# A trunk's second PEER: two dense tiles and two gathered ones in plain float32, U and V rows in one gather

## The chip, the core and the metric

The kernel runs on one core of a Trainium2 chip. The metric is device time in microseconds (us); the time of a kernel is the median of its runs. The engines are TensorE (PE, with its weight loads shown apart as PEld), VectorE (DVE), ScalarE (ACT), GpSimd (POOL) and SyncE (SP). SP and POOL issue nearly all the DMAs, which 16 DMA engines carry out.

## What is computed

The reference is two layers of a transformer-like trunk over 512 latent tokens and 256 context tokens of 1024 features, in float32. Each layer is a mixer (pooling and convolution in layer 0; mLSTM and attention in layer 1) and then PEER, a retrieval of experts, each followed by a residual and a layer norm. In layer 1 only the 512 latent tokens go through PEER, as four tiles of 128 tokens. What PEER computes, cut to what matters:

```python
q = (hb @ w_q).reshape(128, 8, 2, 128)             # 8 heads, two halves of the key
s = einsum('nhpd,pkd->nhpk', q, sub_keys)          # 128 sub-keys for each half
sv, si = top_k(s, 16)                              # then the 16 best of the 16 x 16 sums
eidx, gate = ...                                   # 8 x 16 = 128 experts of 16384 for each token
act = gelu(einsum('nd,nhkd->nhk', hb, u_tab[eidx]))
return einsum('nhk,nhkd->nd', gate * act, v_tab[eidx])
```

The tables U and V have 16384 rows of 1024 float32 each, 64 MB a table. There are two ways to get a token's sum. The dense way multiplies all of U with the tokens, takes the GELU, multiplies by a matrix of gates that is zero except for the chosen experts, and multiplies all of V with that. The gathered way reads only the chosen rows: for each of the 128 choices (a "slot") one indirect DMA brings one row per token, 128 rows in all, and VectorE makes the dot product or adds the weighted row.

## The kernel before

Layer 0 (its mixer and `peer` with l = 0) comes first and the change leaves it as it is. Layer 1 is `mixer1`, whose end is the output projection `proj_out`, and then `peer` with l = 1 (lines 647 to 1100). There three tiles are dense and one (tile 3) is gathered.

Dense products are made with split operands: each float32 operand is cast by ACT to a float32r part (line 297) and DVE makes the remainder (line 298), and TensorE runs three products (hi hi, hi lo, lo hi) in place of one (`mm_chunk`, line 303; line 1070 for V). All PE products show line 69 in the profile, since a helper issues them.

The stages of `peer` in layer 1, in order:

- The query of the gathered tile (lines 926 to 941): 16 pieces of w_q, plain float32, 128 token columns; `scores` (line 705) takes the top 16 of 128 sub-keys on DVE. A piece's scores are issued two pieces later (`QL`).
- The query of the dense tiles and the U products (lines 944 to 972). `u_chunk` (line 911) loads one of 128 chunks of U on SP, splits it, runs 24 products of 384 columns, applies the GELU and stores the result `at` in DRAM (`A_d`). Behind each chunk, `back` (line 892) issues a portion of what the products do not wait for: the choice of experts (`select`, line 725), the gates of the dense tiles (`build`, line 794: ACT and DVE make one-hot rows, PE multiplies them, ACT copies, SP stores 1 MB pieces to `G_d`), and the gathered rows (`run_gather`). A planner's clocks, advanced by the costs in `COST`, decide how much.
- The V products (lines 1034 to 1085): for each chunk SP loads V (two chunks to a DMA), the stored activations (`ag`) and the gates (`gg`); POOL multiplies the two (line 1059), ACT and DVE split both operands, PE adds 18 products of 512 columns into the accumulators `res`. The rest of the gathered rows is spread over these chunks.
- The residual and norm of each tile, and the store of the output (lines 988 to 995).

`gather` (line 662) goes over the table U first, 128 slots of 4 KB rows, then over V, 128 more. POOL issues each indirect DMA (line 667) into one of six row buffers; DVE takes the dot product (line 671) or adds the row (line 675). An instruction on POOL, ACT or DVE waits for all that was issued before it on that engine. In the code, `tc.issue_after` only moves the place of an instruction in that order.

## Time and profile before

| | us |
|---|---|
| median of 3 runs | 3844.92 |
| lowest and highest run | 3842.33, 3851.66 |
| span of the profiled execution | 3842.2 |

No time of its own is listed for the profiled execution, so its span is taken as its time; it lies 2.7 us under the median. The profile gives for each engine the time in which it was busy, for each stretch the mean share in which the 16 DMA engines were busy and the rate in GB/s, and for each group of instructions the count, the busy time and the mean duration. The products are pipelined, so the mean duration of one is longer than the time from one to the next; that is read from the count in a stretch in which PE had no gap. A plain float32 product has two records in the trace, a float32r product one.

### The profile page before, as it was taken

The numbers are of one execution on the slowest core, as the hardware profiler recorded it, in microseconds if no ns is written. First come the engines' busy times: TensorE is split into PE (matmuls) and PEld (weight loads), VectorE is DVE, ScalarE is ACT, GpSimd is POOL, SyncE is SP. The second block draws the span as 40 slices with busy tenths as digits, with TensorE's granted clock in tenths as the row PEclk, the third lists the DMA queues.
The fourth block names the chain that finished last, engine by engine and source line by source line (L and its number), as shares of the span: only waits on it lengthen the run. The fifth ranks groups of instructions, "written<-read, shape, count | busy, mean of one in ns | idle before, by whom it ended". The sixth has DMA issues, their size and how long they took to land. (4 is left out here: it accounts for less than half of the span.)

```text
span 3842.2 us, 57154 instructions
## 1 busy us (share of the span) xinstructions
PE 3659.1 (95%) x20375; PEld 3162.6 (82%) x20375; DVE 3152.0 (82%) x6412; ACT 1836.8 (48%) x3234; POOL 1722.5 (45%) x1225
## 2 busy tenths in 40 slices
PE   7789999999999999999998999899999999999998
PEld 5567877788888778888887888789999999887876
DVE  4877899999999868998886616688999987688778
ACT  4243322378888832322224424533358988333332
POOL 4300055444445557887871203103422223577764
PEclk9899999999999999999999999899999999999999
DMA  5225598889999999999993330157978989888885
GB/s 232 88 91 198 180 326 307 302 319 355 366 344 356 373 338 355 359 367 367 356 342 136 127 127 4 66 192 276 314 263 320 314 290 342 300 318 321 324 314 197
DMA packets 377149, 1044.00 MB, mean 272 GB/s; under 512 B 32288, under 2 KB 171936, under 8 KB 346656
## 3 DMA queue, kind: packets, MB, share of 16 engines
q1 hardware_dynamic: 262960, 619.56, 44.1%
q0 software_dynamic: 113760, 420.53, 30.4%
q8 instruction: 160, 2.62, 0.3%
q14 instruction: 125, 1.02, 0.1%
q10 hardware_dynamic: 144, 0.26, 0.0%
HBM read 915.98 MB, written 124.26 MB: 271 GB/s over the span
## 5 line engine op out<-in xcount | busy, mean ns | idle before, releaser
L667 POOL DMA_INDIRECT g_row<-in_peer_u_dram,g_idx x384 | 529.1, 1378 | 788.5 <-DVE g_row L671 397.0
L667 POOL DMA_INDIRECT g_row<-in_peer_v_dram,g_idx x384 | 576.5, 1501 | 308.0 <-DVE g_acc L675 188.9
L297 ACT CAST c_hi<-c_raw 128x1024 fp32r<-128x1024 f32 x304 | 318.2, 1047 | 593.3 <-PE ups L69 484.4
L298 DVE TENSOR_TENSOR v_lo<-v_raw,v_hi 128x1024 fp32r<-128x1024 f32 x256 | 409.7, 1600 | 214.8 <-ACT v_hi L297 214.5
L297 ACT CAST v_hi<-v_raw 128x1024 fp32r<-128x1024 f32 x256 | 269.3, 1052 | 656.5 <-DMA v_raw<-in_peer_v_dram 380.0
L1059 POOL TENSOR_TENSOR w<-ag,gg 128x512 f32<-128x512 f32 (+1 forms) x256 | 455.2, 1778 | 278.7 <-DVE w_lo L298 234.2
L69 PE MATMUL res<-v_hi,w_hi 128*128 128x512 f32 x1792 | 556.1, 391 | 12.6 <-ACT w_hi L297 12.6
L69 PE MATMUL res<-v_lo,w_hi 128*128 128x512 f32 x1792 | 555.3, 390 | 1.1
L69 PE MATMUL res<-v_hi,w_lo 128*128 128x512 f32 x1792 | 554.5, 390 | 0.0
L675 DVE SCALAR_TENSOR_TENSOR g_acc<-g_row,g_act,g_acc 128x1024 f32<-128x1024 f32 x381 | 533.2, 1399 | 2.2
L298 DVE TENSOR_TENSOR c_lo<-c_raw,c_hi 128x1024 fp32r<-128x1024 f32 x304 | 373.3, 1229 | 147.0 <-ACT c_hi L297 143.9
L671 DVE SCALAR_TENSOR_TENSOR g_row<-g_row,g_h 128x1024 f32<-128x1024 f32 x384 | 488.1, 1288 | 6.2 <-DMA g_row<-in_peer_u_dram,g_idx 6.0
L69 PE MATMUL ups<-opah,c_hi 128*128 128x512 f32 x1152 | 458.5, 398 | 4.9 <-ACT c_hi L297 4.9
L69 PE MATMUL ups<-opah,c_lo 128*128 128x512 f32 x1152 | 453.4, 394 | 9.7 <-DVE c_lo L298 9.4
L69 PE MATMUL ups<-opal,c_hi 128*128 128x512 f32 x1152 | 451.3, 392 | 0.0
L69 PEld LDWEIGHTS res<-v_hi,w_hi 128*128 128x128 f32 x1792 | 336.6, 188 | 85.9 <-ACT w_hi L297 16.7
L69 PEld LDWEIGHTS res<-v_lo,w_hi 128*128 128x128 f32 x1792 | 336.3, 188 | 75.0 <-DVE v_lo L298 5.6
L69 PE MATMUL ups<-opch,c_hi 128*128 128x384 f32 x1152 | 393.7, 342 | 3.7 <-ACT c_hi L297 3.7
L69 PEld LDWEIGHTS res<-v_hi,w_lo 128*128 128x128 f32 x1792 | 336.2, 188 | 71.1 <-DVE w_lo L298 2.0
L69 PE MATMUL ups<-opch,c_lo 128*128 128x384 f32 x1152 | 387.8, 337 | 3.6 <-DVE c_lo L298 3.6
L69 PE MATMUL ups<-opcl,c_hi 128*128 128x384 f32 x1152 | 386.7, 336 | 0.0
L805 ACT ACTIVATE o<-iota,ijT 128x128 f32<-128x128 f32 x896 | 293.0, 403 | 0.2
(469 smaller groups left out, 6699.8 us busy)
## 6 DMA issues: line engine op xcount, KB each, us to landing
c_raw<-in_uT_dram SPq DMA_DIRECT2D x256, 512.0 KB, 6.1
v_raw<-in_peer_v_dram SPq DMA_DIRECT2D x128, 1024.0 KB, 7.7
G_d<-stage SPq DMA_DIRECT2D x56, 1024.0 KB, 7.8
c_raw<-in_peer_wq_dram SPq DMA_DIRECT2D x64, 512.0 KB, 4.9
gg<-G_d SPq DMA_DIRECT2D x64, 512.0 KB, 9.8
A_d<-at SPq DMA_DIRECT2D x120, 256.0 KB, 6.4
ag<-A_d SPq DMA_DIRECT2D x30, 1024.0 KB, 10.9
gg<-G_d SPq DMA_DIRECT2D x64, 384.0 KB, 8.9
```

The lines of the kernel that those rows point to most:

```text
L69: self.last = self.engine.matmul(*args, **kw)
L297: copied[0] = S.copy(hi, src)
L298: return V.tensor_tensor(lo, src, hi.bitcast(F32), op=OP.subtract)
L667: G.indirect_dma_start(out=row, out_offset=None, in_=a[f"peer_{'uv'[tab]}{l}"], in_offset=bass.IndirectOffsetOnAxis(ap=idx[i][:, s:s + 1], ...
L671: V.scalar_tensor_tensor(row, row, 1.0, h, op0=OP.mult, op1=OP.mult, accum_out=w)
L675: V.scalar_tensor_tensor(acc, row, w, acc, op0=OP.mult, op1=OP.add)
L805: S.activation(o1[:, i], iota, AF.Abs, bias=tr[:, 0, n0 + i:n0 + i + 1])
L1059: G.tensor_tensor(w.rearrange("p (t m) -> p t m", m=TG), ag[:, i], gg[:, :, (c + i) % GG, :], op=OP.mult)
```

## The change

The change concerns layer 1 alone. Tiles 0 and 1 stay dense; tile 2 joins tile 3 as a gathered tile. All products there are plain float32 (the output projection too), with no split. U and V of layer 1 are also laid side by side in one table, `peer_uv1`, of 8 KB rows, and one indirect DMA per slot brings both; the GELU of a slot, its weight (two ACT operations on 128x1) and the addition of its V half follow, the addition two slots later (`LAG_G`). A new function `peer_streams` takes the place of `peer`:

- It makes the query of tile 3, its choice of experts in one piece, and the rows of the last gate; then the query of the other three tiles.
- U is streamed in 64 pairs of chunks. The activations of a pair stay in SBUF, in a ring of 15 tiles, and no longer go through DRAM. After 15 pairs the ring is full, and the products wait until the choice of the other tiles and the gates of the dense ones are made (`while front: fill(7.0)`).
- Then pairs of V and pairs of U alternate until U is at its end, and 15 pairs of V follow alone.
- `fill` issues what the products do not wait for. Its clocks go by the costs in `PAY` and in its calls; it issues slots as long as the DVE clock is behind the PE clock. A clock for DMA is kept too, but no condition asks it.

The gates of the dense tiles are made with a comparison and a product in place of one operation for each token, and `G_d` has an order in which a read is one run of 8 KB per partition. The diff, cut to its core:

```diff
--- before
+++ after
+ROWS = 6
+LAG_G = 2
+RING = 15
+FRONT_SHARE = 1.2
...
-    DENSE = ([0, 1, 2, 3], [0, 1, 2])
-    GATH = ([4, 5], [3])
-    ORDER = ([4, 5, 0, 1, 2, 3], [3, 0, 1, 2])
+    DENSE = ([0, 1, 2, 3], [0, 1])
+    GATH = ([4, 5], [3, 2])
+    ORDER = ([4, 5, 0, 1, 2, 3], [3, 2, 0, 1])
...
+    class Whole:
+        def __init__(self, n, name):
+            self.stack = ExitStack()
+            self.pool = pool(self.stack, name, side="right")
+            self.t = self.pool.tile([P, KB, n], F32, name=name)
+        def room(self, shape, name):
+            return self.pool.tile(shape, F32, name=name)
+        def cols(self, t):
+            return self.t[:, :, t * P:(t + 1) * P]
...
+        hf = (op.cols(t) if l else wp.tile([P, KB, P], F32, name="hf", bufs=2) if dense else
               gt["acc"][:, GATH[l].index(t)].rearrange("p (b n) -> p b n", n=P))
...
+            h = gt["hs"][GATH[l].index(t)] if l else gt["h"][:, GATH[l].index(t)]
+            S.copy(h[:, b0 * P:(b0 + n) * P], ps.rearrange("p b n -> p (b n)"))
...
+        pairs = [(op.t, wts[0])] if l else [(op.hi, wts[0]), (op.hi, wts[1]), (op.lo, wts[0])]
...
-                for m, w, first, last in ((op.hi, wh, k == 0, False), (op.hi, wl, False, False),
-                                          (op.lo, wh, False, k == KB - 1)):
+                for i, (m, w) in enumerate(pairs):
                     for h in range(2):
                         PE.matmul(ps[:, h * 512:(h + 1) * 512], m[:, k, sl], w[:, k, h * 512:(h + 1) * 512],
-                                  start=first, stop=last)
+                                  start=k + i == 0, stop=(k, i) == (KB - 1, len(pairs) - 1))
...
-        ng = len(GATH[l])
+        ng = 1 if l else len(GATH[l])
...
+        G_d = dr.tile([P, NCHUNK // GG, ntg, GG, TG], F32, name=f"G_d{l}")
...
+        def scores(m, ps, tiles):
+            nt = len(tiles)
+            qT = wp.tile([P, nr], F32, name="qT", bufs=2)[:, :nt * P]
+            S.copy(qT, ps)
+            ps2 = pp.tile([P, 4, P], F32, name="scps", tag="misc", bufs=4)
+            for i in range(nt):
+                PE.matmul(ps2[:, i], qT[:, i * P:(i + 1) * P], keys[:, m % 2], start=True, stop=True)
+            for i, t in enumerate(tiles):
+                src = ps2[:, i]
+                si = wp.tile([P, TOPK], U32, name="si", bufs=2)
+                s2 = wp.tile([P, P], F32, name="s2", bufs=2)
+                V.max(sv[:, t, m, 0:8], src)
+                V.max_index(si[:, 0:8], sv[:, t, m, 0:8], src)
+                V.match_replace(s2, sv[:, t, m, 0:8], src, NEG)
+                V.max(sv[:, t, m, 8:16], s2)
+                V.max_index(si[:, 8:16], sv[:, t, m, 8:16], s2)
+                V.tensor_copy(sib[:, t, m], si)
+                yield "score"
...
+        def build(t):
+            tr, jb = chosen.pop(t)
+            sh = [P, W8, P]
+            for g in range(P // TG):
+                stg = wp.tile([P, P, TG], F32, name="stage", bufs=2)
+                for b in range(TG // W8):
+                    n0 = g * TG + b * W8
+                    nb = slice(n0, n0 + W8)
+                    o1 = wp.tile(sh, F32, name="o1", bufs=2)
+                    oe = wp.tile(sh, BF16, name="oe", bufs=2)
+                    o2 = wp.tile(sh, F32, name="o2", bufs=2)
+                    for i in range(W8):
+                        S.activation(o1[:, i], iota, AF.Abs, bias=tr[:, 0, n0 + i:n0 + i + 1])
+                    S.activation(o1, o1, AF.Relu, bias=1.0, scale=-1.0)
+                    V.tensor_tensor(oe, iotab.unsqueeze(1).to_broadcast(sh), jb[:, nb].unsqueeze(2).to_broadcast(sh),
+                                    op=OP.is_equal)
+                    V.tensor_tensor(o2, oe, tr[:, 2, nb].unsqueeze(2).to_broadcast(sh), op=OP.mult)
+                    for i4 in range(0, W8, W4):
+                        pq = pp.tile([P, W4, P], F32, name="gps", tag="misc", bufs=4)
+                        for i in range(W4):
+                            PE.matmul(pq[:, i], o1[:, i4 + i], o2[:, i4 + i], start=True, stop=True)
+                        n1 = b * W8 + i4
+                        S.copy(stg[:, :, n1:n1 + W4].rearrange("p i n -> p n i"), pq)
+                    yield "build"
+                tg = (dense.index(t) * P) // TG + g
+                SP.dma_start(G_d[:, :, tg], stg.rearrange("p (q c) m -> p q (c m)", c=GG))
...
+        def gather(i):
+            acc, h = accs[i], gt["hs"][i]
+            late = []
+            def add(s, row, w):
+                if s == 0:
+                    V.tensor_scalar(acc, row[:, D:], w, None, op0=OP.mult)
+                else:
+                    V.scalar_tensor_tensor(acc, row[:, D:], w, acc, op0=OP.mult, op1=OP.add)
+            for s in range(P):
+                row = gp.tile([P, 2 * D], F32, name="g_row", bufs=ROWS)
+                G.indirect_dma_start(out=row, out_offset=None, in_=a[f"peer_uv{l}"],
+                                     in_offset=bass.IndirectOffsetOnAxis(ap=idx[i][:, s:s + 1], axis=0))
+                d, w = (gp.tile([P, 1], F32, name=f"g_{z}", bufs=4) for z in "dw")
+                V.scalar_tensor_tensor(row[:, :D], row[:, :D], 1.0, h, op0=OP.mult, op1=OP.mult, accum_out=d)
+                S.activation(d, d, AF.Gelu)
+                S.activation(w, d, AF.Copy, scale=gate[i][:, s:s + 1])
+                late.append((s, row, w))
+                if len(late) > LAG_G:
+                    add(*late.pop(0))
+                yield "slot"
+            for args in late:
+                add(*args)
...
+        PAY = {"score": (1.75, 0, .25), "cand": (1.14, 0, 0), "top": (1.25, 0, 0), "top2": (.85, 0, 0), "eq": (1.4, 0, 0),
+               "tree": (1.05, 0, 0), "gates": (1.0, 0, .6), "build": (2.0, 1.5, 1.8), "slot": (2.75, 2.65, 0)}
...
+        def choice():
+            yield from select(dense[0])
+            for t, u in zip(dense, [*dense[1:], gath[1]]):
+                gens = [build(t), select(u)]
+                while gens:
+                    for q in list(gens):
+                        kind = next(q, None)
+                        if kind is None:
+                            gens.remove(q)
+                        else:
+                            yield kind
...
+        def fill(pe, dma=0.0):
+            clock["pe"] += pe
+            clock["dma"] = max(clock["dma"], clock["pe"] - 12.0) + dma
+            clock["dve"] = max(clock["dve"], clock["pe"] - 12.0)
+            while clock["dve"] < clock["pe"]:
+                first = front and (state["front"] <= 0 or state["slots"] >= P or not slots)
+                if not (front or slots):
+                    break
+                kind = next((front if first else slots)[0], None)
+                if kind is None:
+                    (front if first else slots).clear()
+                    continue
+                pay(kind)
+                state["front"] += PAY[kind][0] * (1 if first else -FRONT_SHARE)
...
+        for m in range(16):
+            raw = query(m)
+            ps = pp.tile([P, 512], F32, name="ups", bufs=4)
+            for k in range(KB):
+                PE.matmul(ps[:, :P], raw[:, k], h1[:, k], start=k == 0, stop=k == KB - 1)
+            for _ in scores(m, ps[:, :P], gath[:1]):
+                pass
+            if m == 7:
+                op.tail(pp)
...
+        for _ in select(gath[0]):
+            pass
+        gate_rows(pg, l, 40, 0, wp, pp, "misc", 4)
+        rp = pool(es, "ps_r", side="right")
+        rest = [*dense, *gath[1:]]
+        clock["dve"] = clock["pe"] = clock["dma"] = 0.0
+        for m in range(16):
+            raw = query(m)
+            ps = pp.tile([P, 512], F32, name="ups", bufs=4)
+            for k in range(KB):
+                PE.matmul(ps[:, :nr], raw[:, k], op.t[:, k, :nr], start=k == 0, stop=k == KB - 1)
+            for kind in scores(m, ps[:, :nr], rest):
+                pay(kind)
+            fill(5.2, 1.3)
+        front.append(choice())
+        ring, u = [], 0
+        NP = NCHUNK // 2
...
+        def u_pair(pool_, tag, bufs):
+            nonlocal u
+            raw = rp.tile([P, 2, KB, P], F32, name="u_raw", bufs=3)
+            SP.dma_start(raw, a[f"uT{l}"][u])
+            ps = pool_.tile([P, 2, n], F32, name="ups", tag=tag, bufs=bufs)
+            for i in range(2):
+                for k in range(KB):
+                    PE.matmul(ps[:, i], raw[:, i, k], op.t[:, k, :n], start=k == 0, stop=k == KB - 1)
+            at = rp.tile([P, 2, n], F32, name="at", bufs=RING)
+            S.activation(at, ps, AF.Gelu)
+            ring.append(at)
+            u += 1
+            fill(6.95, 2.65)
+        while u < RING and front:
+            u_pair(pp, "ups", 4)
+        while front:
+            fill(7.0)
+        ef.close()
...
+        for j in range(NP):
+            c = 2 * j
+            if c % GG == 0:
+                gg = vp.tile([P, ntg, GG, TG], F32, name="gg", bufs=2)
+                SP.dma_start(gg, G_d[:, c // GG])
+            v = vp.tile([P, 2, D], F32, name="v_raw", bufs=2)
+            SP.dma_start(v, vv[:, c:c + 2])
+            w = vp.tile([P, 2, n], F32, name="w", bufs=2)
+            if not ring:
+                u_pair(pp, "ups", 8 - 2 * nd)
+            at = ring.pop(0)
+            for i in range(2):
+                G.tensor_tensor(w[:, i].rearrange("p (t m) -> p t m", m=TG), at[:, i].rearrange("p (t m) -> p t m", m=TG),
+                                gg[:, :, c % GG + i], op=OP.mult)
+            ops = w, v
+            if j < NP - 2:
+                for i in range(2):
+                    for t in range(nd):
+                        mm(ops, c, i, t)
+            else:
+                tail.append((ops, c))
+            fill(6.85, 3.4)
...
+            if u < NP:
+                u_pair(pp, "ups", 8 - 2 * nd)
...
-                    split(op.hi[:, b4, sl], op.lo[:, b4, sl], ps)
+                    (V.tensor_copy if half else S.copy)(op.t[:, b4, sl], ps)
...
-                wts = load_wout(a["cd_w_out"], wo, po, "rl_tmp")
+                wts = [wo.tile([P, KB, D], F32, name="wo")]
+                for k in range(KB):
+                    SP.dma_start(wts[0][:, k], a["cd_w_out"][k * P:(k + 1) * P])
...
-        peer(op, 1, gt, out.rearrange("(t p) d -> t p d", p=P))
+        peer_streams(op, 1, gt, out.rearrange("(t p) d -> t p d", p=P))
...
-    o["uT"] = np.ascontiguousarray(f["peer_u"].reshape(2, P, NCHUNK, KB, P).transpose(0, 2, 4, 3, 1))
-    for l in range(2):
-        o[f"peer_u{l}"], o[f"peer_v{l}"] = f["peer_u"][l], f["peer_v"][l]
+    uT = f["peer_u"].reshape(2, P, NCHUNK, KB, P).transpose(0, 2, 4, 3, 1)
+    o["uT"] = np.ascontiguousarray(uT[:1])
+    o["uT1"] = np.ascontiguousarray(uT[1].reshape(NCHUNK // 2, 2, P, KB, P).transpose(0, 2, 1, 3, 4))
+    o["peer_u0"], o["peer_v0"], o["peer_v1"] = f["peer_u"][0], f["peer_v"][0], f["peer_v"][1]
+    o["peer_uv1"] = np.concatenate([f["peer_u"][1], f["peer_v"][1]], 1)
...
```

## Rows read from the trace of the kernel before

**Rows 1.** Stretches: busy PE, PEld, DVE, ACT, POOL, clock, DMA share, GB/s.

```profile
2450.00:2520.00 70.00, 68.27 (x384) 56.67 (x382) 38.96 (x79) 24.16 (x42) 0.62 (x1) 1.00 0.18 61
2520.00:2572.00 52.00, 47.63 (x365) 46.40 (x366) 49.29 (x208) 16.15 (x35) 1.63 (x3) 0.93 0.72 250
2572.00:3290.00 718.00, 703.73 (x4288) 690.39 (x4287) 616.13 (x1588) 482.71 (x896) 215.29 (x163) 1.00 0.84 294
3290.00:3826.00 536.00, 526.59 (x2290) 429.89 (x2289) 428.92 (x383) 187.00 (x255) 379.95 (x222) 0.99 0.84 306
3826.00:3842.00 16.00, 2.61 (x12) 1.84 (x10) 12.73 (x30) 0.41 (x2) 0.00 (x0) 0.70 0.25 98
```

**Rows 2.** The same columns, 25 us of U and of V products.

```profile
2800.00:2825.00 25.00, 25.00 (x146) 25.00 (x145) 24.54 (x63) 10.53 (x14) 2.08 (x2) 1.00 0.74 253
3300.00:3325.00 25.00, 25.00 (x112) 20.71 (x111) 19.40 (x18) 6.17 (x9) 20.26 (x13) 1.00 0.93 326
```

**Rows 3.** Plain float32 products: tile invn, then tile ups in 5 us.

```profile
L69 PE MATMUL zps<-cacc,invn x16: 378/485/668, 240.3 to 245.3; 128*128 128x512 f32 x8, 128*128 128x256 f32 x8
345.00:350.00 5.00, 5.00 (x25) 4.41 (x24) 0.39 (x2) 1.00 0.80 258
```

**Rows 4.** Groups by form, 2520 to 3842, PE: count, busy us, mean ns.

```profile
L69 PE MATMUL ups<-g_acc,c_raw 128*128 128x128 f32 x256 | 33.1, 287 | 0.0
L69 PE MATMUL gps<-o,o 128*128 128x128 f32 x768 | 100.9, 277 | 5.6 <-ACT o L806 5.4
```

**Rows 5.** The same view, DVE: score, choice and rows.

```profile
L716 DVE MAX8 sv<-scps 128x8 f32<-128x128 f32 x64 | 18.8, 293 | 0.0
L717 DVE MATCH_VALUE_LOAD si<-sv,scps 128x8 f32 x64 | 5.3, 83 | 0.4
L737 DVE TENSOR_TENSOR candd<-sv 128x1024 f32<-128x1024 f32 x6 | 7.3, 1222 | 0.0
L744 DVE FIND_INDEX8 posd<-topd,candd 128x8 uint32<-128x256 f32 x24 | 10.1, 420 | 0.0
L762 DVE TENSOR_TENSOR eqd<-eqd,sib 128x1024 bf16<-128x1024 bf16 x12 | 8.3, 696 | 0.2
L766 DVE TENSOR_TENSOR eqd<-eqd 128x512 bf16<-128x512 bf16 x12 | 5.1, 423 | 0.1
L671 DVE SCALAR_TENSOR_TENSOR g_row<-g_row,g_h 128x1024 f32<-128x1024 f32 x128 | 154.2, 1216 | 1.8 <-DMA g_row<-in_peer_u_dram,g_idx 1.7
L671 DVE DVE_READ_ACCUMULATOR g_row<-g_row,g_h 128x1 f32 x128 | 10.8, 84 | 0.0
L675 DVE SCALAR_TENSOR_TENSOR g_acc<-g_row,g_act,g_acc 128x1024 f32<-128x1024 f32 x127 | 162.0, 1275 | 0.2
```

**Rows 6.** The same view, ACT and POOL.

```profile
L805 ACT ACTIVATE o<-iota,ijT 128x128 f32<-128x128 f32 x384 | 125.1, 402 | 0.1
L806 ACT ACTIVATE o<-o 128x512 f32<-128x512 f32 x96 | 60.8, 633 | 1.9
L814 ACT COPY stage<-gps 128x512 f32<-128x512 f32 x96 | 102.0, 1076 | 0.1
L708 ACT COPY qT<-ups 128x384 f32<-128x384 f32 x16 | 7.5, 469 | 0.0
L1059 POOL TENSOR_TENSOR w<-ag,gg 128x384 f32<-128x384 f32 x128 | 222.5, 1739 | 164.4 <-DVE w_lo L298 126.8 <-PE ups L69 32.0 <-DVE rl_s L217 4.2
L667 POOL DMA_INDIRECT g_row<-in_peer_v_dram,g_idx x128 | 204.7, 1599 | 93.9 <-DVE g_acc L675 53.2 <-DVE g_acc L673 10.8 <-issue 8.0
```

**Rows 7.** DMA, 2520 to 3842; one issue (KB, us to landing); two stretches.

```profile
DMA packets 146233, 389.97 MB, mean 295 GB/s; under 512 B 11695, under 2 KB 76207, under 8 KB 134869
v_raw<-in_peer_v_dram SPq DMA_DIRECT2D x64, 1024.0 KB, 8.0
1400.00:2000.00 600.00, 600.00 (x2649) 496.95 (x2648) 526.94 (x490) 178.79 (x227) 490.20 (x300) 1.00 0.96 362
1600.00:1625.00 25.00, 25.00 (x112) 20.72 (x111) 20.77 (x20) 8.06 (x11) 19.21 (x13) 1.00 1.02 410
```

More of the change, by code (lines that the diff above doesn't have):

```diff
@@ L346, in peer_hT @@
             turn(hf, wide(n), xt, t, *mod, b0=b0)
-            yield hf if dense else None
+            yield hf if dense and l == 0 else None
         for b0 in range(0, 0 if dense else KB, n):
@@ L401, in proj_out @@
             V.tensor_tensor(xn, xn, like(lb, xn), op=OP.add)
[L402 removed]
+            G.dma_start(x_d[2 * l][t] if l else x_d[2 * l][t].rearrange("p (b n) -> p b n", n=P), xn)
         def tail(pp):
+            hf = op.cols(t) if l else spare[1]
             for b0 in range(0, KB, 4):
[L406 removed]
+                turn(hf, pp.tile([P, 4, P], F32, name="hps", tag="misc", bufs=4), xn, t,
                      modT[l][:, 32:40], modT[l][:, 24:32], b0=b0)
[L408 removed]
+            if l == 0:
+                parts_of(op, t, hf)
         op.tail = tail
@@ L630, in hps @@
                 return pp.tile([P, n, P], F32, name="hps", bufs=2)
-            for _ in proj_out(op, 0, *wts, xsrc, gt, wp, proj_rows(0, wp, pp, ("hps", 2)), wops, hps, KB, (5, 7)):
+            for _ in proj_out(op, 0, wts, xsrc, gt, wp, proj_rows(0, wp, pp, ("hps", 2)), wops, hps, KB, (5, 7)):
                 pass
@@ L1340, in mixer1 @@
             pre.close()
-            op = Operand(NL, "opc", len(DENSE[1]) * P)
+            op = Whole(NL, "opc")
+            gt["hs"] = [gt["h"][:, 0], op.room([P, D], "g_h1")]
             with ExitStack() as e2:
@@ L1594, in mixer1 @@
                 state["quad"] = quad
-                proj = proj_out(op, 1, *wts, x_d[1], gt, po, rows, wops, quad, 4, LAGS)
+                proj = proj_out(op, 1, wts, x_d[1], gt, po, rows, wops, quad, 4, LAGS)
                 need, count, busy = None, 0, True
```

163 lines of the change are left out of this document (154 added, 9 removed).

## The prediction

> **What bounds the kernel now.** I read the stretches of the second PEER first, since the change leaves the rest alone up to the projection before it. From 2520 us to the end at 3842 us PE is busy for nearly all of the U stretch (703.7 of 718 us) and of the V stretch (526.6 of 536), while DMA has a share of 0.84 in both [rows 1]. So PE bounds both, and the 25 us stretches give its prices: 146 products of 384 columns in 25 us are 0.171 us each, so 24 of them make a U chunk of 4.1 us; 112 of 512 columns are 0.223 us each, and 18 make a V chunk of 4.0 us [rows 2]. DMA is not idle beside it: 390 MB go through in these 1322 us [rows 7]. The reader should see that PE is the bound, but that the next one is near.
>
> **The products.** What plain float32 costs is seen in the trace. Sixteen records of 512 and 256 columns start within 5.0 us, and 25 records of 256 columns run in 5 us [rows 3]: that is 0.83 ns a column, so 0.213, 0.320 and 0.427 us for 256, 384 and 512 columns, two records a product. (At 128 columns a record takes 33.1/256 = 0.129 us, and a product of the gate builds 2 x 100.9/768 = 0.26 us [rows 4].) A pair of U chunks is then 32 x 0.213 = 6.8 us, a pair of V chunks 16 x 0.427 = 6.8 us, against 8.2 and 8.0 us now. PE gains some 80 us in V and 90 us in U; the splits on ACT and DVE go, which hid beside PE and give nothing by themselves.
>
> **The bytes.** A slot brings 128 rows of 8 KB, 1.05 MB, and there are 256 of them: 268 MB in place of 134 MB. What goes is the activations' way through DRAM (120 chunks of 196 KB, twice: 47 MB) and a third of the gates, written and read (17 MB). U, V and the two passes of w_q stay. So 390 MB become some 460 MB, and the question is whether they come at times when DMA is free.
>
> Rates: the long stretch in layer 0 with V loads and 4 KB gathered rows ran at 362 GB/s with a share of 0.96, and one 25 us stretch at 410 with a share of 1.02 [rows 7]. That is 377 at a full share, 410 at best. The new traffic has longer runs than the stretch at 362, so I take 390 and keep 362 and 410 as ends. The Trainium skill ("DMA: Bandwidth & Descriptors", Specifications) puts the HBM limit of a core at about 358 GB/s. The row at 410 exceeds that, so the sum does not go by it; by 358 it would be some 65 us longer.
>
> **The sum**, stage by stage, on the clock of the profiled execution.
>
> *Projection, to 2525.* It is bound by PE now (68.3 of 70 us [rows 1]). 192 products of 0.223 us become 128 records of 0.427 us: 43 us become 55, and eight more transposes come. Against it the weights are no longer split before use, nor the operand. I take +5 us, between -5 and +14.
>
> *Query of tile 3 and its choice, 84 us.* Sixteen pieces of 16 records, 2.1 us each, but now PE waits in each for the copy of the query (0.47 us at 384 columns, less here [rows 6]) before the score product, since scores are no longer held back: 2.6 us, 42 us in all. The tail's transposes and turns add 4. Then `select` of tile 3 runs on DVE with nothing issued beside it. From [rows 5]: two sums of 1.22, eight times five searches of 0.42 and three loads of 0.08, eight operations of 0.70, four trees of some 1.3, and 1 for the gates: 33 us. The diagonal products of `gate_rows` stand behind it on DVE, and all further queries behind these on PE: 5 us more. Before, this choice lay beside U chunks. Ends: 68 and 92.
>
> *Query of three tiles, 104 us.* Per piece PE has 16 x 0.320 + 6 x 0.131 = 5.9 us and the wait for the copy, 0.6; DVE has three scores of 1.9 (five searches of 0.29, the loads, a small conversion) and a third of a slot. PE is just the longer: 16 x 6.5. Ends: 95 and 115. It ends at 2713. I went through `fill` with its own costs to see where slots fall: 5 here, 62 until the gates are ready, 189 behind that.
>
> *Choice and gates, 350 us.* PE has only 15 pairs of U (102 us) and 64 builds of 1.05 us, then the ring is full and it waits. DVE sets the pace: 62 slots of 1.22 + 0.08 + 1.28 = 2.58 us are 160 us [rows 5], three choices are 99 us, and 64 builds. The two operations of a build on 512 elements are not in the trace; the nearest rows are 0.42 us for 512 bf16 elements and half of 1.28 us for 1024 float32, so 0.85 to 1.28 us the pair; since one side is float32 I take 1.2, 77 us. The sum is 336 us. ACT has 64 x (4 x 0.40 + 0.63 + 1.08) = 212 us [rows 6] and stays beside it, but a slot's GELU queues behind a build there, and DVE behind that two slots later: 14 us for such waits. Ends: 313 and 400. DMA (98 MB, 250 us) is hidden here.
>
> *Opening of the V stage, 10 us.* Its tiles take the room of the choice, so the first load (8.0 us to landing now [rows 7]) and the first gates start behind it. Ends: 0 and 20.
>
> *V and U with slots, 738 us.* By `fill`, the 189 slots go out with 38 pairs of V and 38 of U, five to a period of 13.7 us of PE. These are 198 MB of rows and 90 MB of U, V and gates: 288 MB, which take 738 us at 390 GB/s, 702 at 410, 795 at 362. PE would need 519 us, DVE 488. So DMA sets this stage, a period of 19.4 us. PE cannot run ahead: the multiplication that makes its operand stands on POOL behind the slots' DMAs, each of which waits for one of six row buffers, and the GELU of U stands on ACT behind the slots' GELUs. POOL itself has 5 x 1.6 + 2 x 1.2 = 10 us a period [rows 6] and is hidden; if 8 KB rows doubled the 1.6, 18 us, still under.
>
> *Rest, 253 us.* 26 pairs of V and 11 of U without slots, 6.83 us each, PE-bound. The norms of the gathered tiles lie beside them on DVE. *End, 16 us*, as now.
>
> 2525 + 84 + 104 + 350 + 10 + 738 + 253 + 16 = 4080. The runs' median lies 2.7 us over the span, so **4083 us**, 6% slower. SP issues fewer DMAs than before and waits on nothing that PE is not waiting for; that I cost at nothing.
>
> **The rivals.**
>
> *DMA keeps the rate of layer 0* (362 GB/s): the mixed stage takes 795 us, 4140 in all. For it: that rate already had a share of 0.96. Against: the stretch at 410. By the skill's 358 it would be 4149. Chance 0.20.
>
> *The choice stage is held by the coupling of ACT, DVE and PE* rather than by DVE's sum: 420 us, 4153 in all. Chance 0.08.
>
> *DMA hides the gathers*: the mixed stage goes at PE's 519 us, 3864 in all, still slower, because the choice of tile 3 and the gates stand open. It would need 555 GB/s, far over any row. Chance 0.08.
>
> *The other side, faster:* PE and the loads are not held by the slots, so DMA never stops from the choice stage on. Then 431 MB from 2713 on decide: 1051 us at 410, so 3783; 1105 at 390, so 3837. The point is some 392 GB/s held for all that time. For it: the bytes in total would fit. Against: the order on POOL, and the DVE-bound choice stage, whose 98 MB do not fill DMA. Chance 0.09.
>
> **How the numbers follow.** My forecast has 0.55. About 0.3%, 12 us, is what a measurement of this kernel can tell from no change. The two cases on the slow side and the forecast are slower; of the last rival two thirds are faster, the rest within 0.3%, and of "DMA hides the gathers" half would be faster or the same with the other terms at their short ends. That makes 0.09 faster, 0.04 same, 0.87 slower. The range takes in the ends of the terms, not all at once, and the two slow rivals: 3950 to 4190. It leaves out the two fast ones, 0.17.
>
> **What would show it.** In the profile after: a PE busy share of about one half between the query and the first V product, with DVE near full; then some 740 us with a DMA share near 1 and about 390 GB/s, PE with a gap of 5 us in each period, 3.9 us from slot to slot; then 250 us of full PE with DMA at half its share. Wrong it is if PE has no gaps in the mixed stage (DMA carried it), if DMA has a share well under 0.9 there while PE waits (the buffers' cycle sets it, not the rate), or if the choice stage is far from 350 us.

## The result, and the profile after

The changed kernel takes 3968.14 us (median of 4 runs, 3964.34 to 3972.09), the kernel before 3844.83 beside it (3842.33 to 3851.66): a ratio of 1.0313, between 1.0296 and 1.033. It is slower by 123 us; the forecast was 4083, 115 us too long. The profiled execution has a span of 3969.2 us.

The second PEER by stages, in the view of stretches (columns as in [rows 1]):

```profile
2466.00:2540.00 74.00, 72.75 (x278) 40.12 (x277) 32.10 (x68) 19.64 (x37) 1.19 (x2) 1.00 0.20 79
2540.00:2597.00 57.00, 40.56 (x305) 37.16 (x306) 42.70 (x197) 7.20 (x22) 1.07 (x2) 0.88 0.55 192
2597.00:2695.00 98.00, 96.50 (x357) 58.95 (x356) 96.41 (x529) 19.86 (x39) 9.34 (x9) 1.00 0.45 169
2695.00:3015.00 320.00, 217.70 (x1007) 192.85 (x1006) 302.12 (x612) 219.99 (x547) 101.03 (x63) 0.72 0.85 300
3015.00:3040.00 25.00, 16.90 (x73) 14.32 (x71) 13.62 (x18) 3.56 (x14) 6.90 (x7) 0.84 1.00 380
3040.00:3727.00 687.00, 587.78 (x1889) 379.53 (x1890) 476.21 (x560) 112.07 (x407) 351.75 (x260) 0.92 1.01 418
3727.00:3956.00 229.00, 220.56 (x630) 120.20 (x629) 13.29 (x21) 9.39 (x14) 33.84 (x46) 0.98 0.43 156
3956.00:3969.20 13.20, 0.57 (x2) 0.00 (x0) 9.61 (x24) 0.20 (x1) 0.00 (x0) 0.65 0.20 79
```

The lines are the projection, the query of tile 3 with its choice, the query of three tiles, choice and gates, the opening of V, V and U with slots (the mixed stage), the rest, and the end. Before, PE had 24 us of gaps in the 1254 of U and V, and DMA a share of 0.84 [rows 1]. Now there is a long stage in which DMA's share is 1.01 and PE has 99 us of gaps (687 less 588), and a rest in which PE is full and DMA at 0.43. Most of the loss is that these two do not lie beside each other; e8 below shows how much.

What the mixed stage moved, from the view of DMA over 3040 to 3727 us (packets; then issues, count and median us to landing):

```profile
DMA packets 39706, 287.14 MB, mean 418 GB/s; under 512 B 4416, under 2 KB 4416, under 8 KB 4928
...
u_raw<-in_uT_dram SPq DMA_DIRECT2D x40, 1024.0 KB, 9.7
v_raw<-in_peer_v_dram SPq DMA_DIRECT2D x38, 1024.0 KB, 9.1
...
g_row<-in_peer_uv_dram,g_idx POOLq DMA_INDIRECT x181, 17.1
```

181 slots go out with 38 pairs of V and 40 of U, 4.7 to a pair of each. And who waits there, from the waits of PE, DVE, ACT and POOL in the same stretch (total us, times, longest):

```profile
PE ups L73 <- ACT at L1392: 71.3, 20, 9.9
PE res L73 <- POOL w L1435: 25.5, 7, 8.2
PE res L73 <- DMA v_raw<-in_peer_v_dram: 10.4, 3, 8.1
...
DVE g_acc L1282 <- ACT g_w L1291: 114.6, 177, 8.8
DVE g_row L1289 <- DMA g_row<-in_peer_uv_dram,g_idx: 104.3, 78, 5.4
...
ACT g_d L1290 <- DVE g_row L1289: 568.8, 181, 8.0
...
POOL g_row L1286 <- DVE g_acc L1282: 285.5, 137, 4.9
```

PE waits for a transfer of its own, a V load, for only 10 us. For the rest it waits for the GELU of U (71 us), which stands on ACT behind the slots' GELUs, and for the products on POOL (26 us), which stand behind the slots' DMAs. ACT's 569 us stand at the head of its queue, for a DVE pass that in turn waits for a row. So the rate of the rows reaches PE through two queues. The chain that ended last, from 2695 us on, has 32.8% of its time in the landing of rows:

```profile
by line: DMA g_row<-in_peer_uv_dram,g_idx 32.8%; issue 14.7%; PE res L73 13.5%; DVE g_acc L1282 6.2%; PE ups L73 5.1%; POOL g_row L1286 5.1%; PE gps L73 3.6%; DVE g_row L1289 3.4%; ACT stage L1267 2.0%; DVE o L1261 1.8%; DVE oe L1259 1.6%; 
...
3014.88 17.20 DMA G_d<-stage
3032.60 7.18 DMA v_raw<-in_peer_v_dram
3039.92 9.72 PE res L73 x16
```

Its middle lines are the opening: the last write of the gates (17.2 us) and the first V load that the chain goes through (7.2 us) make up 24 of its 25 us.

### The profile page after: what moved, and what is told of

It reads as the page before. It is cut to its first block, busy times and chain, and to the rows that moved or that the text cites. A ratio compares the mean times of both kernels' runs of the same rounds, so it can differ in the third digit from the quotient of the medians.

```text
span 3969.2 us, 50277 instructions
## 1 busy us (share of the span) xinstructions
PE 3577.8 (90%) x17628; PEld 2792.2 (70%) x17628; DVE 2995.8 (75%) x6151; ACT 1515.4 (38%) x3080; POOL 1639.6 (41%) x1225
## 5 line engine op out<-in xcount | busy, mean ns | idle before, releaser
L1286 POOL DMA_INDIRECT g_row<-in_peer_uv_dram,g_idx x256 | 359.9, 1406 | 674.4 <-DVE g_acc L1282 531.5
L73 PE MATMUL ups<-opc,u_raw 128*128 128x256 f32 x2048 | 483.3, 398 | 71.3 <-ACT at L1392 71.3
L73 PEld LDWEIGHTS ups<-opc,u_raw 128*128 128x128 f32 x2048 | 408.2, 201 | 157.7 <-ACT at L1392 88.3
L73 PE MATMUL res<-v_raw,w 128*128 128x512 f32 x1024 | 460.3, 606 | 44.4 <-POOL w L1435 25.5
L1282 DVE SCALAR_TENSOR_TENSOR g_acc<-g_row,g_w,g_acc 128x1024 f32<-128x1024 f32 x254 | 333.8, 1314 | 114.8 <-ACT g_w L1291 114.6
L73 PE MATMUL gps<-o,o 128*128 128x128 f32 x1536 | 244.1, 318 | 113.3 <-ACT o L1258 47.1
L73 PEld LDWEIGHTS gps<-o,o 128*128 128x128 f32 x1536 | 227.6, 226 | 139.9 <-ACT o L1258 55.8
L73 PE MATMUL res<-v_hi,w_hi 128*128 128x512 f32 x1024 | 316.6, 390 | 2.1 <-ACT w_hi L318 2.1
L73 PE MATMUL res<-v_hi,w_lo 128*128 128x512 f32 x1024 | 316.4, 390 | 0.0
L73 PE MATMUL res<-v_lo,w_hi 128*128 128x512 f32 x1024 | 316.3, 390 | 0.0
```

Source lines behind the costliest of these rows:

```text
L73: self.last = self.engine.matmul(*args, **kw)
L1282: V.scalar_tensor_tensor(acc, row[:, D:], w, acc, op0=OP.mult, op1=OP.add)
L1286: G.indirect_dma_start(out=row, out_offset=None, in_=a[f"peer_uv{l}"], in_offset=bass.IndirectOffsetOnAxis(ap=idx[i][:, s:s + 1], axis=0))
```

## The experiments

Twelve kernels, each an edit of the changed one. In the profiles of kernels whose code up to there is the same, the projection's first product stands between 2455 and 2468 us; so single looks are compared by the length of their stages, and the whole only where it differs by more than that.

### What sets the mixed stage

**e1_half_rows**: a slot gathers 4 KB, the V row alone, for both passes.

```diff
-G.indirect_dma_start(out=row, ..., in_=a[f"peer_uv{l}"], ...)
+G.indirect_dma_start(out=row[:, :D], ..., in_=a[f"peer_v{l}"], ...)
-V.scalar_tensor_tensor(acc, row[:, D:], w, acc, ...)
+V.scalar_tensor_tensor(acc, row[:, :D], w, acc, ...)
```

> The slots gather 4 KB rows of V alone and use them for both operations on VectorE; the U half of the rows is left out, all instructions stay. If the DMA rate sets the mixed stage (3040 to 3727 us, 421 GB/s): its 288 MB become 189 MB, 450 us at that rate, less than the 519 us of PE, so the stage falls from 687 to 520 to 550 us and the whole to about 3810 to 3840. If the cycle of the six row buffers and the order on GpSimd set it, whatever the size: the stage stays over 620 us, the whole over 3900. If PE sets it: no change, about 3968.

One look: 3932.18 us. The mixed stage and the rest, in stretches:

```profile
3028.00:3588.00 560.00, 482.49 (x1529) 300.06 (x1530) 464.92 (x558) 109.89 (x401) 340.18 (x248) 0.93 0.85 310
3588.00:3917.00 329.00, 318.37 (x990) 188.67 (x989) 13.62 (x21) 13.01 (x21) 41.57 (x58) 0.98 0.46 163
```

The mixed stage falls by 127 us (687 to 560) and is no longer full (310 GB/s). But the rest grows by 100 us (229 to 329): the slots stand closer on GpSimd's queue (180 with 32 V loads, 5.6 to a pair), so less of PE's work lay beside them. The code emits them as before, so I put that down to the framework's schedule; no run shows its reason. By the whole, the theory of the rate would have fallen; by the stage it stands, at 10 us over its forecast. The whole was the wrong thing to forecast. What holds the stage at 560 us, 3.1 us to a slot, was not tested: DMA, PE (482 us) and VectorE (465 us) all have time left, and PE now waits for the w products on POOL for 75 us.

**e2_half_u**: PE does half the contraction of U.

```diff
-for k in range(KB):
-    PE.matmul(ps[:, i], raw[:, i, k], op.t[:, k, :n], start=k == 0, stop=k == KB - 1)
+for k in range(KB // 2):
+    PE.matmul(ps[:, i], raw[:, i, k], op.t[:, k, :n], start=k == 0, stop=k == KB // 2 - 1)
```

> Half of the contraction blocks of the U products are left out, the loads stay. PE has 3.4 us less for each pair of U. If DMA sets the mixed stage: it stays within 15 us of 687, and only the rest behind it loses 9 to 11 pairs x 3.4 us, so the whole is about 3930 to 3940. If PE sets the mixed stage: it loses 38 x 3.4 = 129 us too, the whole about 3800.

One look: 3945.07 us.

```profile
2695.00:3015.00 320.00, 181.23 (x773) 155.42 (x772) 303.62 (x629) 220.40 (x549) 93.82 (x64) 0.61 0.86 301
3043.00:3727.00 684.00, 483.33 (x1231) 280.58 (x1232) 474.17 (x560) 112.46 (x407) 347.39 (x260) 0.85 1.00 417
3727.00:3930.00 203.00, 196.39 (x515) 98.29 (x513) 12.59 (x21) 9.22 (x14) 32.73 (x46) 0.98 0.49 176
```

PE loses 104 us of work in the mixed stage and the stage keeps its length; the stage of choice keeps its 320 us too. Only the rest is shorter; the whole is 5 us over what was expected. PE's work on U sets neither of the two. It doesn't clear PE of the builds, though: the granted clock of the stage of choice fell from 0.72 to 0.61 (more on the clock at e7).

**e3_two_gathers**: two indirect DMAs of 4 KB rows for one of 8 KB.

```diff
-G.indirect_dma_start(out=row, ..., in_=a[f"peer_uv{l}"], ...)
+for h_, z_ in enumerate("uv"):
+    G.indirect_dma_start(out=row[:, h_ * D:(h_ + 1) * D], ..., in_=a[f"peer_{z_}{l}"], ...)
```

> Each slot's 8 KB rows come as two gathers of 4 KB rows from U and from V, the same bytes. If the length of the runs is what let the rate be 421 GB/s and not the 377 that layer 0 bears out: the mixed stage goes from 687 us towards 764, the whole to 4000 to 4050. If the run length does not matter: the stage stays within 10 us, the whole at about 3970, or some us more where GpSimd's 10 issues of 1.4 us come near the period of 18 us.

One look: 3984.04 us.

```profile
3050.00:3700.00 650.00, 539.27 (x1762) 343.76 (x1760) 435.08 (x519) 102.76 (x373) 515.90 (x408) 0.93 1.02 410
```

The same bytes in shorter runs go at 410 GB/s. That is the very rate and share of the one 25 us stretch before [rows 7]; the longer run is worth 2 to 3%, no more. The 181 slots go out with the same 38 and 40 pairs, from 3038 to 3740 us: 702 us, 15 more than in the change, a little over the 10 of the second forecast and far from the 764 of the first. GpSimd is busy for 516 us of these 650, where the change has 336, and DMA is still full.

### Whether the rest can be covered

**e4_paced**: the slots of the V stage are held to 3.5 for a pair of V and U and 1.6 for a pair of V, where the code emits them.

```diff
-if not (front or slots):
+if not (front or slots) or not first and state["slots"] >= state["cap"]:
...
+state["cap"] = state["slots"]
...
+state["cap"] += 1.75 if u < NP else 1.6
...
+    state["cap"] += 1.75
```

> From the first V product on, slots are issued at an even pace, 3.5 to a pair of V and U and 1.6 to a pair of V alone, in place of 5 until they end. If DMA sets the mixed stage and lies half idle in the rest: all bytes from the first V product on, 333 MB, take 791 us at 421 GB/s, and PE needs 772 us, so that stretch goes from 941 us to some 800 to 830 and the whole to 3830 to 3860. If the slots' own cycle or PE set the stage, the slots' spreading gives less than 40 us.

Three rounds: 3925.28 us, ratio 1.0188 (1.0171 to 1.0205), 43 us under the change and far over what was expected.

```profile
3050.00:3725.00 675.00, 608.47 (x2029) 390.95 (x2027) 455.37 (x530) 106.86 (x386) 350.87 (x260) 0.95 1.01 421
3755.00:3917.00 162.00, 152.40 (x415) 79.16 (x415) 12.94 (x19) 7.12 (x10) 25.20 (x34) 0.97 0.45 162
```

DMA is still full and a rest of 162 us is left: in the order of GpSimd's queue 4.2 slots go out per pair, since the framework brings them forward of where they are emitted. So the next run holds them on the queue itself.

**e8_paced_anchor**: e4, and each slot of the V stage is tied behind the last w product on GpSimd.

```diff
-kind = next((front if first else slots)[0], None)
+with tc.issue_after(anchor[-1].ins) if anchor and not first else nullcontext():
+    kind = next((front if first else slots)[0], None)
...
-G.tensor_tensor(w[:, i]..., op=OP.mult)
+anchor.append(G.tensor_tensor(w[:, i]..., op=OP.mult))
```

> The changed kernel with the slots really spread over the V stage: at most 3.5 of them to one pair of V and one of U, 1.6 to a pair of V alone, and each held on GpSimd's queue behind the w product of its pair, so that the framework can't bring it forward (in the run paced without that hold, 4.2 went out per pair). Theory that the rate of 421 GB/s sets the mixed stage and that PE's 808 us in 3040 to 3956 were left for last: one pair of V, one of U and 3.5 slots are 5.8 MB, 13.7 us at 421 GB/s, as long as PE's products; the stages of V go by PE, about 3040 to 3860, little is left after the last slot, and the whole is 3855 to 3895. Theory that the slots' own cycle (row buffer, the two passes of VectorE, GpSimd's issue) sets it, whatever the pace: the whole stays at 3910 or more, with DMA under 400 GB/s in 3100 to 3700.

Three rounds: 3864.92 us, ratio 1.0032 (1.0016 to 1.0047).

```profile
3050.00:3700.00 650.00, 620.15 (x2110) 403.49 (x2109) 414.88 (x487) 102.29 (x362) 307.37 (x246) 0.97 1.01 421
3700.00:3800.00 100.00, 89.62 (x246) 46.66 (x245) 64.83 (x76) 14.86 (x55) 52.90 (x43) 0.98 0.96 390
```

103 us of the 123 are back (by the ratios to the kernel before beside each, 1.0313 and 1.0032, nine tenths of the loss) with no operation changed, only the place of the slots: DMA's 421 GB/s and PE's 95% now stand in the same stretch. The slots themselves go out slower than in the change (165 from 3031 to 3700 us, 4.1 us each, for 3.8) and DMA's rate is the same, so the slots' own cycle, the rival, is not what held them.

### What sets the stage of choice

**e5_pool_o2**: one of the two DVE operations of each build goes to GpSimd.

```diff
-V.tensor_tensor(o2, oe, tr[:, 2, nb].unsqueeze(2).to_broadcast(sh), op=OP.mult)
+G.tensor_tensor(o2, oe, tr[:, 2, nb].unsqueeze(2).to_broadcast(sh), op=OP.mult)
```

> The changed kernel with one instruction of the builds moved: the product o2 (bf16 matrix of ones times the gate) runs on GpSimd instead of VectorE, 64 of them, 689 ns each on VectorE. It tells what sets the stage of choice and gates (2695 to 3015 us, 320 us, VectorE busy for 302 of it). If VectorE does: 64 x 0.69 = 44 us of its work go, the stage is 275 to 285 us, the first V product stands at 2995 to 3005, and the whole falls to 3925 to 3940. If the stage is held by something else (the landing of rows, ScalarE's share of the builds, or GpSimd now late with the gathers that stand behind the products): 310 us or more, and the whole stays at 3960 to 3980.

One look: 3987.99 us; the builds take 270 us from first product to last, against 258. The groups of the stage (2695 to 3015 us), first of the change, then of this run:

```profile
L1282 DVE SCALAR_TENSOR_TENSOR g_acc<-g_row,g_w,g_acc 128x1024 f32<-128x1024 f32 x64 | 82.2, 1284 | 0.0
L1289 DVE SCALAR_TENSOR_TENSOR g_row<-g_row,g_h 128x1024 f32<-128x1024 f32 x64 | 78.1, 1221 | 1.7 <-DMA g_row<-in_peer_uv_dram,g_idx 1.7
...
L1261 DVE TENSOR_TENSOR o<-oe,ijT 128x512 f32<-128x512 bf16 x64 | 43.6, 689 | 14.4 <-PE gps L73 14.3
L1259 DVE TENSOR_TENSOR oe<-iotab,jT 128x512 bf16<-128x512 bf16 x64 | 42.8, 688 | 0.0
```

```profile
L1282 DVE SCALAR_TENSOR_TENSOR g_acc<-g_row,g_w,g_acc 128x1024 f32<-128x1024 f32 x61 | 91.0, 1492 | 8.3 <-ACT g_w L1291 8.3
...
L1261 POOL TENSOR_TENSOR o<-oe,ijT 128x512 f32<-128x512 bf16 x63 | 81.4, 1296 | 74.3 <-PE gps L73 42.2 <-DVE oe L1259 17.9 <-DVE c L1191 7.9
L1289 DVE SCALAR_TENSOR_TENSOR g_row<-g_row,g_h 128x1024 f32<-128x1024 f32 x58 | 77.6, 1339 | 6.8 <-DMA g_row<-in_peer_uv_dram,g_idx 6.7
...
L1259 DVE TENSOR_TENSOR oe<-iotab,jT 128x512 bf16<-128x512 bf16 x63 | 48.2, 777 | 15.1 <-POOL o L1261 15.1
```

VectorE got slower beside GpSimd's products: 1492 ns for 1284, 1339 for 1221, 777 for 688; its searches of one operand (MAX8) did not, 411 ns for 430. That takes back about half of the 44 us (61 x 0.208 + 58 x 0.118 + 63 x 0.089 = 25); more went into waits (oe for the product on GpSimd, 15 us). The Trainium skill ("GPSIMD Engine Reference", 1. Specifications) has GpSimd contend with VectorE instructions of two SBUF inputs; the trace agrees, all three have two and a MAX8 has one. So this run alone can't say whether VectorE sets the stage.

**e13_act_o2** asks it without GpSimd. (It stands on e12, below; the edit is in the builds only.)

```diff
+if b % 4 == 3 or (g % 3 == 1 and b == 1):
+    for i in range(W8):
+        S.activation(o2[:, i], oe[:, i], AF.Copy, scale=tr[:, 2, n0 + i:n0 + i + 1])
+else:
     V.tensor_tensor(o2, oe, ...)
```

> The same with 22 of the 64 products o2 of the builds done by ScalarE, four activations of 394 ns each, in place of VectorE's one of 689 ns. VectorE loses 22 x 0.69 = 15 us in the stage of choice, ScalarE gains 35 us there (220 busy of 320 before), and neither shares anything with GpSimd. Theory that VectorE sets that stage, one for one: the first V product 12 to 16 us sooner than with the third V buffer alone, and the whole that much less, 3830 to 3846. Theory that the chain of ScalarE, PE and VectorE through the builds sets it: within 5 us of the third V buffer alone, or slower.

Three rounds: 3864.95 us, ratio 1.0039 (1.0028 to 1.005), 8 us over e12, where 12 to 16 less would have shown VectorE. The builds' products, first and last, in the view of the tile:

```profile
L73 PE MATMUL gps<-o,o x512: 272/421/583, 2749.2 to 3037.4; 128*128 128x128 f32 x171
```

288 us, where e12 had 267. Over the builds VectorE was busy for 11 us less (231 for 242) and ScalarE for 22 more (224 for 202), and they took 21 longer.

**e7_front_first**: builds and choices before slots, so that 10 slots pass VectorE between the builds in place of 52.

```diff
-first = front and (state["front"] <= 0 or state["slots"] >= P or not slots)
+first = front
```

> The changed kernel with the order of the planner turned in the stage of choice alone: builds and choices first, no slot as long as there are any; 27 slots stand before the first w on GpSimd's queue in place of 75. It tells what the builds cost by themselves: 258 us from their first product to their last with slots between, VectorE busy for 240 of it and ScalarE for 200. Theory that VectorE sets them: without some 48 slots of 2.6 us it has 125 us less, and the builds take 135 to 175 us. Theory that ScalarE sets them with VectorE and PE in a chain (each of 64 builds is four activations of 394 ns, one of 628 and a copy of 1035 on ScalarE, 3.24 us): 205 to 230 us, so that a slot there costs under 1.1 us of stage. The slots go to the stages of V at 2.5 us each by DMA: by the first theory the whole is 3950 to 3985, by the second 4010 to 4060.

One round: 3933.64 us, ratio 1.0207 (1.0178 to 1.0237). The tile of the builds' products, then a stretch in their midst:

```profile
L73 PE MATMUL gps<-o,o x512: 273/275/582, 2737.6 to 2940.0; 128*128 128x128 f32 x171
```

```profile
2750.00:2850.00 100.00, 94.15 (x525) 76.54 (x524) 91.69 (x230) 99.07 (x220) 4.57 (x4) 1.00 0.65 212
```

With 10 slots between them the builds take 202 us, near ScalarE's sum (64 x 3.24 = 207), and ScalarE is busy for 99 of 100 us there. With 52 they take 258: 42 slots cost 56 us, 1.3 us each, half of their 2.6 us on VectorE.

But not all of that need be the slots' work. The granted clock of TensorE differs too: its mean over the builds is 0.80 here (2738 to 2940 us) and 0.66 in the change. Later in the builds of e7, with the U products before the V stage done, PE is busy for 29 of 50 us at a clock of 0.50 (1.2 GHz), and ScalarE is not full. First that stretch of e7, then the products of a build at a clock of 1.00 (2.4 GHz), the same at 0.50, and the copy on ScalarE behind them; last, the end of the builds in the change:

```profile
2863.00:2913.00 50.00, 29.06 (x112) 24.94 (x112) 18.78 (x28) 36.05 (x85) 0.00 (x0) 0.50 0.25 77
...
2797.05 1.16 PE L73 MATMUL gps<-o,o 128*128 128x128 f32 x8
...
2867.39 2.08 PE L73 MATMUL gps<-o,o 128*128 128x128 f32 x8 [1.54 <-ACT o L1258]
2869.51 1.03 ACT L1267 COPY stage<-gps 128x512 f32<-128x512 f32 x1 [1.01 <-PE gps L73]
...
2905.00:3013.00 108.00, 50.29 (x198) 44.08 (x199) 105.78 (x197) 81.21 (x200) 36.38 (x23) 0.50 0.83 283
```

At half the clock the eight records of a build take 2.08 us in place of 1.16, ScalarE stands 1.01 us in each build waiting for them, and from one build to the next it is 3.62 us (2865.89 to 2869.51), where it was 2.7 to 3.0. So no one engine holds the stage: ScalarE does where the clock is full and slots are few, the loop of ScalarE and PE in e7 where the clock is half, and VectorE at the end of the change's builds (106 of 108 us). VectorE's work moved to ScalarE (e13) or to GpSimd (e5) makes it no shorter. Nothing was taken off ScalarE, and no run holds the clock, so how the 56 us divide stays open.

Both forecasts of the whole were too long: they priced the slots moved to V at 2.5 us each, but they also cover PE's rest, which is 87 us here in place of 229.

### Whether both kernels can be beaten

**e9_paced_anchor_pool** is e8 with the edit of e5.

> The held spread and the move of o2 to GpSimd together. If VectorE sets the stage of choice and DMA the stage of V, their gains add: 35 to 45 us under the run with the held spread alone, 3815 to 3855, that is level with the kernel before or under it. If the stage of choice is not VectorE's: the same as the held spread alone, within 10 us. If only one of the gains stands, because the slots that the shorter stage of choice can't take go to the V stage: 10 to 25 us under it.

Three rounds: 3878.29 us, ratio 1.0067 (1.005 to 1.0084), 13 over e8. The gain is not there, and VectorE's three groups are as long as in e5 (1501, 1357 and 775 ns).

**e10_ring20** is e8 with a longer ring and five row buffers, **e11_open** the same with seven slots ahead of the first w, **e12_v3** is e10 with a third V buffer in place of the third U buffer:

```diff
-ROWS = 6
+ROWS = 5
-RING = 15
+RING = 20
... e11 beside it
+for _ in range(7):
+    next(slots[0])
+opened.append(gathered[-1])
... e12 beside e10
-raw = rp.tile([P, 2, KB, P], F32, name="u_raw", bufs=3)
+raw = rp.tile([P, 2, KB, P], F32, name="u_raw", bufs=2)
-v = vp.tile([P, 2, D], F32, name="v_raw", bufs=2)
+v = vp.tile([P, 2, D], F32, name="v_raw", bufs=3)
```

> The held spread with a ring of 20 activations in place of 15 and five row buffers in place of six (the ring's 10 KB per partition come from the row buffer). Five more pairs of U are computed in the stage of choice, where PE stands idle for a third of the time and DMA isn't full. Theory that the stages of V go by DMA's 421 GB/s beside PE: five U pairs less there are 35 us of PE and 5.2 MB, 12.5 us of DMA; the stage of choice keeps its 320 us (VectorE sets it), the first V product stands at 3030 to 3040, and the whole is 3820 to 3850. Theory that six rows in flight are needed to fill the queue: DMA falls under 400 GB/s in 3100 to 3600 and the whole is 3860 or more.

> The ring of 20 with five row buffers, and seven slots put on GpSimd's queue before the first w product of the V stage, which stood on that queue for 34.5 us (the wait for the read of G behind its last write), with no gather going out for 35 us. Theory that DMA's bytes set the stages of V: seven slots, 7.3 MB, go out in a stretch where DMA was half idle, 10 to 17 us less than the ring of 20 alone, 3805 to 3835. Theory that VectorE is the limit there (its 2.6 us for each slot) or that the first w comes later by them: level with the ring of 20 alone, or slower by up to 10.

> The held spread with a ring of 20, with a third buffer for the V rows (8 KB, taken from the U rows, which keep two of three). In the run with the ring of 20, from 3700 us on, where only V is left beside the slots, neither engine nor queue is full: PE is busy for 92% and DMA moves 365 GB/s, while SP's loads of V wait for PE to free a buffer. Theory that the landing of a V load, behind the slots' rows, is longer than the one product that covers it: with three buffers PE is busy for 97% or more in 3650 to 3800, and the whole falls by 8 to 15 us, to 3845 to 3858. Theory that PE waits there for something else (w, GpSimd's queue) or that bytes set the end: no change, within 4 us.

e10: 3864.39 us (1.0032, 1.0019 to 1.0045), no gain over e8, though five rows in flight carry 418 GB/s. Five more U pairs in the stage of choice make the builds 268 us in place of 257, so it doesn't keep its length as expected. From the first V product to the last it takes 797 us, 20 less than e8; the way to the first V product takes 9 of them back, and the end 12: 25 us from the last V product to the end of the kernel, where e8 has 13. And from 3700 us on neither PE nor DMA is full:

```profile
3050.00:3650.00 600.00, 568.74 (x1925) 368.63 (x1924) 384.15 (x449) 93.88 (x332) 287.89 (x227) 0.97 1.01 418
3700.00:3800.00 100.00, 91.54 (x202) 38.62 (x201) 52.16 (x61) 9.95 (x40) 47.71 (x44) 0.97 0.92 365
```

e11: 3860.69 us (1.0021, 1.0005 to 1.0037), level with e10 within the intervals. From the last product of the builds to the first of V it takes 25 us, where e10 takes 17, and the time from the first V product to the last is 799 us as against 797: the slots that went early did not shorten it. e12: 3857.09 us (1.0009, 0.9999 to 1.0019), 7 less than e10, with the stretch full:

```profile
3700.00:3800.00 100.00, 100.00 (x235) 44.24 (x234) 60.26 (x69) 11.45 (x46) 57.34 (x52) 1.00 1.01 419
```

That is the theory of the landing, at one us short of what it named. e12 is level with the kernel before (3852.20 beside it); no run beat it. In e12 DMA moves 419 of its 421 GB/s in both stretches that were shown of e10, with PE at 95% in the first (567 of 600 us) and at 100% in the second. The V products gained more than the whole, 778 us for 797 (e10, then e12):

```profile
L73 PE MATMUL res<-v_raw,w x1024: 592/592/1221, 3028.6 to 3825.9; 128*128 128x512 f32 x171
L73 PE MATMUL res<-v_raw,w x1024: 592/592/1222, 3042.1 to 3820.2; 128*128 128x512 f32 x171
```

For now the last slots come behind PE. In e12 the last of them is added at 3833 us, 13 us after PE's last V product; with the norms of their tile behind them on VectorE the kernel ends 32 us after that product, where the change and e8 take 13. What is left to gain is at the two ends of the V stages: that tail, which no run tried to shorten, and the builds, beside which DMA moves 297 GB/s. Between them there is little left to fill.

## Why the prediction was right, and where it was off

The direction and the mechanism of the mixed stage held: DMA's rate sets V and U with slots, PE is held through POOL's and ACT's queues, and what it can't do there comes after. The predicted 189 slots, 38 pairs and 288 MB of that stage are 181, 38 to 40 and 287 MB. e2 shows that PE's work on U doesn't set it, e3 that GpSimd's issue doesn't, e8 that the slots' buffers don't. The gap of PE in a period was 2.6 us (99 over 38 pairs) for a forecast 5, the rate being higher. Stage by stage the terms were 141 us too long and 30 too short; that they partly cancel is luck. (That is 111 of the 115; the rest is the profiled execution beside the median.)

*The rate, 51 us of the 141.* 738 us were forecast at 390 GB/s, 687 were measured at 418. The failed step is "377 at a full share": 362 GB/s at a share of 0.96 was divided by the share, and 410 taken as the upper end. But the stretch at 362 was one in which PE was full [rows 7]; DMA was not asked for more. The full queue was seen only in the 25 us at 410 and a share of 1.02, and e3, with the same 4 KB rows, runs at 410 for 650 us. The row was a price, not an upper end; 8 KB rows then bring 421. The rival at 362 falls with it. The 358 GB/s by which the prediction had an alternative sum are what each core gets when both cores of a pair stream, as another page of the Trainium skill says ("HBM Reference", Specifications (TRN2)); for a core that streams alone it has about 425. The trace agrees with that one: this kernel runs on one core, at 418 over 687 us.

*Choice and gates, 30 us.* The terms were counted nearly right: 64 slots, the pair of a build's operations 1.38 us for a forecast 1.2. The failed step is the sum of 336 us: it laid mean durations end to end. The stage's 612 VectorE instructions have durations that add up to 350.6 us, and the engine was busy for 302.1: each overlaps the next by 0.08 us. (The Trainium skill, "Perfetto Trace Analysis", Optimizing Scalar/DVE Operations, says that the half of an instruction's access time in which its write is acknowledged overlaps the next instruction; the trace agrees in that they overlap.) The rival with the coupling, 420 us, did not come; but a milder coupling is there (e7, e13), and "DVE sets the pace" is only half true: it does at the end of the builds, and with fewer slots it is ScalarE. PE was busy for 0.68 of the stage where the prediction named about one half: its products were priced at the full clock, and the granted one was 0.72 there.

*Choice of tile 3, 27 us.* 57 us for 84. The failed step is "with nothing issued beside it". In the timeline of VectorE and PE, the searches of the choice stand between those of the last score pieces, and the next query runs before the choice is done:

```profile
2594.40 0.42 DVE L1193 MAX8 top<-c 128x8 f32<-128x256 f32 x1
2594.73 0.28 DVE L1164 MAX8 sv<-s 128x8 f32<-128x128 f32 x1
...
2595.67 6.62 PE L73 MATMUL ups<-opc,q_raw 128*128 128x384 f32 x20
...
2596.57 0.42 DVE L1194 FIND_INDEX8 pos<-top,c 128x8 uint32<-128x256 f32 x1
```

L1193 and L1194 belong to `select`, the rest to the pieces. I had read the order of the code as the order of the engines' queues.

*The rest, 24 us, and the small terms.* 253 us became 229: PE got some four pairs further by then than `fill`'s clocks said, I take it in the longer opening and in the gaps. The query of three tiles took 98 us for 104, the end 13 for 16. The opening took 25 for 10: I had priced the first load, not the write of the last gates behind which their reading stands. The projection took 72 us from first product to last, 12 more than the 60 before, where 5 more were forecast, and began at 2466 where it had begun at 2459; as said above, that start moves by 13 us from one execution to the next. So it ended at 2540 for a forecast 2525.

*The rivals.* "The other side" put the point at 392 GB/s from the choice stage to the end. That rate came in the mixed stage alone; from 2695 to 3956 us the mean is 340. The rival needed two things: the rate, and slots that don't hold PE. e8 gave the second and came to 3865, not 3783 to 3837, because the stage of choice keeps its 320 us and moves 289 GB/s there. "DMA hides the gathers" named 3864, and e8 came to 3865; that is chance. It has 772 us for the V stages, which took 817 in e8, and its other terms were too long by as much; and its reason was wrong: DMA did not get faster, its bytes were spread.

## What to carry to other kernels

When two limits, here DMA's bytes and PE's products, each fill a stage while the other idles, the cure here was not a faster part but the same parts in another order; the size of the prize was about the idle time of PE in both stages together (99 and 8 us, and e8 got 103). A pace set where the code emits an instruction holds only if something on its queue holds it too. A stage's length says what an edit did; the whole can hide 127 us of gain behind 100 us of work uncovered elsewhere. And before an engine's busy time is called the bound, look at what it waits for and at the granted clock.

## What the runs showed of the hardware that I had not expected

Beside 1 MB loads, DMA goes at 421 GB/s for 650 us on end with 8 KB rows and at 410 with 4 KB rows. VectorE's products with two operands take up to 16% longer (1284 to 1492 ns) while GpSimd multiplies 512 elements beside them. In the builds TensorE's granted clock was 0.50 for long, and there, in e7, ScalarE waited 1 us in every build for products that took 2.08 us in place of 1.16. And durations of VectorE in the trace overlap: 612 of them add up to 48 us more than the engine was busy.
